# Pooling mixer of a diffusion trunk: rows scaled on ScalarE, the shift added by short matrix products

## The chip, the cores and the metric

The kernel runs on one core of a Trainium2 chip. The metric is the device time of one execution in microseconds (us); lower is better. TensorE is called PE in the rows below (PEld is its loading of the stationary operand), VectorE DVE, ScalarE ACT, GpSimd POOL, and SP is the queue that issues the loads.

## What is computed

Two layers over 512 latent tokens of width 1024 (and 256 context tokens in the first): layer 0 mixes tokens by attention, layer 1 by a pooling mixer, and each is followed by a gated feed-forward with a convolution. The change touches the seam from the feed-forward of layer 0 to that of layer 1, where this is computed:

```python
def rmsnorm(x, g):                       # over the 1024 channels of a token
    y = x * rsqrt(mean(x * x) + EPS); return y * g
def modulate(h, shift, scale): return h * (1.0 + scale) + shift

# layer 1, mixer: h = modulate(rmsnorm(x, g_pre_mix), shift_m, scale_m)
# four groups of 256 channels, windows w = 2, 4, 8, 16
pooled = mean of h over [t - w/2, t + w/2) (clipped to the sequence) - h[t]
y = (pooled @ w_pool[g] + b_pool[g]) * pool_scale
x = x + gate_m * rmsnorm(y, g_post_mix)
h = modulate(rmsnorm(x, g_pre_ffn), shift_f, scale_f)      # input of the second feed-forward
```

For a token in the middle of the sequence the window weights sum to one, so mean minus token gives zero for anything that is the same at every token, the shift among it. Within 8 tokens of either end that need not hold.

## The kernel before

Tokens lie in four tiles t of 128 partitions (`x[0]` to `x[3]`, full precision); the eight PSUM banks are four pairs `B2[0]` to `B2[3]` (printed as b1, b2, b3, b0 in this order). The second product of the first feed-forward (`down(0, ...)`, lines L122 to L124, three products of the split halves of both operands for each block) ends tile after tile, and `after_ffn0(t)` follows each:

- `post_norm` (L249 to L254): squares of the row on ScalarE (L167), the mean on VectorE (L168, L169), the power -1/2 on GpSimd (L151), then the residual is added on VectorE (L251, L254).
- the pre-norm of layer 1: again L167, L168, L169 and L151, then on VectorE `h = x * Arow` (L876, two halves of 512 columns) and `h = h * r + Brow` (L878, two halves). `Arow` and `Brow` hold gain and shift, copied to all 128 partitions by `to_row` (L207).
- `band(half, s)` (L844): products of `hx[s]` with columns of `bandt`, a matrix that holds the window weights minus one on the diagonal, with different columns for the first, the inner and the last tile. They run in full precision, and the trace has two records for each: 46 products in the program, 92 records.
- `pooled(half)` splits the sums into two parts `hTp` (cast on ScalarE, L128; rest on VectorE, L129). `mix(t)` multiplies with the pool weights (L122 to L124) and adds the bias (L861), then does `post_norm`. `mixed(t)` is `pre_norm(t, ...)` for the second feed-forward: L167 to L151, row scaling on VectorE (L231, into `mixrow`), eight transposes on TensorE (L234), gain and shift on VectorE for the first half (L239) and on ScalarE for the second (L242), and the split into `hT` (L128, L129), on which the first products of the second feed-forward (`up7`) wait.

After tile 3 come `mix(0)`, `mix(1)`, the remaining bands, `pooled(1)`, `mixed(0)`, `mixed(1)`, `mix(2)` and `mix(3)`; `mixed(2)` and `mixed(3)` are called inside `up7`. A scheduler of the framework places the instructions on each engine's queue; each queue runs in order.

Of the kernel before, what the change touches and what calls it, by code (L numbers as in the profile page):

```python
# [13 lines left out]
AF = mybir.ActivationFunctionType  # L14
ALU = mybir.AluOpType
AX = mybir.AxisListType

P = 128
D = 1024
SEQ = 512  # L20
CTX = 256
KT = D // P
TT = SEQ // P
# [15 lines left out]

HALO = 8  # L40

BI, BE = P + 2 * HALO, P + HALO
BW = BI + 2 * BE
NSLOT = 64

PE_TILE = 5
# [3 lines left out]
def trunk(ctx: ExitStack, tc: tile.TileContext, a, out: bass.AP):  # L50
    nc = tc.nc
# [35 lines left out]
    def rows(name, i, n=2, dt=F32):  # L87
        return flat(slots(name, i, n, dt))
# [111 lines left out]
    def gate_col(i, n):  # L200
        V.tensor_mul(Gcol[:, i, n, :], mods[:, i, 3 * n + 2, :], gcols[:, 2 + n, i, :])

    def to_row(dst, col):

        d = dram.tile([KT, P], F32, tag="bounce", name="bounce")
        nc.sync.dma_start(out=d.rearrange("j p -> p j"), in_=col)
        nc.sync.dma_start(out=dst, in_=d.rearrange("j p -> (j p)").unsqueeze(0).broadcast_to([P, D]))  # L207

    bg = []

# [10 lines left out]
    def halves(z):  # L221
        return [z[:, c] for c in HALVES]

    def pre_norm(t, pair, xn, A, Bc, h32=h32):


        r = rstd_halves(halves(x[t]), xn)
        ps = [z.rearrange("p (j s) -> p j s", s=P) for z in pair]
        sl = slice(t * P, (t + 1) * P)
        for c in range(2):  # L230
            V.tensor_scalar(xn[:, HALVES[c]], x[t][:, HALVES[c]], r, None, op0=ALU.mult)  # L231
            for j in range(4):
                f = 4 * c + j
                T.transpose(ps[c][:, j, :], xn[:, f * P:(f + 1) * P], ident)  # L234
        for c in range(2):
            for j in range(4):
                f = 4 * c + j
                if c == 0:
                    V.tensor_scalar(h32[:, f, :], ps[c][:, j, :], A[:, f:f + 1], Bc[:, f:f + 1],  # L239
                                    op0=ALU.mult, op1=ALU.add)  # L240
                else:
                    S.activation(h32[:, f, :], ps[c][:, j, :], AF.Identity, bias=Bc[:, f:f + 1], scale=A[:, f:f + 1])  # L242
        for c in range(2):
            k = slice(4 * c, 4 * c + 4)
            split(hT[:, k, sl], hT[:, KT + 4 * c:KT + 4 * c + 4, sl], h32[:, k, :])
# [552 lines left out]
    Gm1 = flat(cvt)  # L798
    hall = slots("hall", 52, KT, F32)
    wpl_dst = [[rows(f"wpl{n}{z}", i + 2 * z, dt=F32R) for z in range(2)] for n, i in enumerate((16, 20))]  # L800
    Arow, Brow = rows("Arow", 24), rows("Brow", 26)
    bandt = rows("band", 28, 4)[:, :4 * BW].rearrange("p (g b) -> p g b", g=4)
    hTp = [[slots(f"hTp{n}{z}", (32, 44)[n] + 4 * z, 4) for z in range(2)] for n in range(2)]
    wtail = [tuple(rows(f"wtail{n}{z}", 4 * n + 2 * z, dt=F32R) for z in range(2)) for n in range(4)]
# [24 lines left out]
    def band(half, s, groups=range(4)):  # L829
# [8 lines left out]
        for g in groups:  # L838
            if at == 256 and g == 0:
                continue  # L840
            ps = B2[2 * half + g // 2][g % 2].rearrange("p (k s) -> p k s", k=2)
            for k in range(2):
                f = slice((2 * g + k) * P, (2 * g + k + 1) * P)
                T.matmul(ps[:, k, lo:hi], hx[s][:, f], bandt[:, g, b0:b0 + hi - lo],  # L844
                         start=at == 0 and k == 0, stop=False, skip_group_check=True)

    def pooled(half):
        hi, lo = (z.rearrange("p a (j s) -> p (a j) s", s=256) for z in hTp[half])
# [15 lines left out]
        mixrow.append(row)  # L864

    def mixed(t):
        pre_norm(t, B2[t], mixrow[t], Acol[:, 1, 1], mods[:, 1, 3], hall[:, :, t * P:(t + 1) * P])

    def after_ffn0(t):
        if t == 1:  # L870
# [4 lines left out]
        for c in HALVES:  # L875
            V.tensor_mul(h[:, c], x[t][:, c], Arow[:, c])  # L876
        for c in HALVES:
            V.scalar_tensor_tensor(h[:, c], h[:, c], r, Brow[:, c], op0=ALU.mult, op1=ALU.add)  # L878
        hx.append(h)
        if t == 1:  # L880
            band(0, 0)
# [20 lines left out]
    def each0(c, kk):  # L902
# [5 lines left out]
            ps_row.append(pool_bias())  # L908
        if c == 1 and kk == FT // 2 - LAST:
            to_row(Arow, Acol[:, 1, 0, :])  # L910
            to_row(Brow, mods[:, 1, 0, :])
            pool_weights(ps_row[0])

    def down(i, aT, done, each, last, dst=(), order=(2, 3, 0, 1)):
# [32 lines left out]
def _constants():  # L947

    f = np.float32
# [14 lines left out]
    for g, w in enumerate(WINDOWS):  # L964
# [2 lines left out]
        e = m - np.eye(SEQ, dtype=f)  # L967
        band[:, g, :BI] = e[P:2 * P, P - HALO:2 * P + HALO]
        band[:, g, BI:BI + BE] = e[:P, :BE]
        band[:, g, BI + BE:] = e[SEQ - P:, SEQ - BE:]  # L970
    return rope, band


# [53 lines left out]
```

## Time and profile before

| | |
|---|---|
| runs | 1074.54, 1069.29, 1071.18 us; median 1071.18 |
| profiled execution | 1074.04 us, of which the span from first to last instruction is 1072.3 |
| busy share of the span | PE 93%, VectorE 70%, ScalarE 48%, GpSimd 3% |
| chain that ended last | PE 56%, VectorE 18%, DMA 12%, ScalarE 8% |
| mean granted TensorE clock | 0.977 of full speed |

The profiled execution is 2.86 us above the median of the runs. A difference that is worked out on its trace is therefore added to the median. The seam that the change touches lies between 648 and 730 us of the span.

### The profile page before, as it was taken

To read this page: it belongs to the slowest core of one execution; us is meant where nothing else is said; L and a number is where in the kernel's file an instruction comes from. 1 tells how busy PE (TensorE), PEld (TensorE's weight loads), DVE (VectorE), ACT (ScalarE), POOL (GpSimd) and SP (SyncE) were. 2 spreads that over 40 slices of the span, in tenths; PEclk is the share of its full clock that TensorE was granted. 3 is DMA by queue.
4 is the path that set the end of the run, shared out by engine and by line. 5 is a ranking of instruction groups with operands and counts; after the bars stand their busy time and mean duration, and the time that the engine had idled before them with its cause. 6 is when DMAs were issued, how large, how long until landed. Compare 5 with 4: busy or idle time off the path is not lost.

```text
span 1072.3 us, 14605 instructions
## 1 busy us (share of the span) xinstructions
PE 997.8 (93%) x5586; PEld 862.9 (80%) x5586; DVE 747.6 (70%) x1259; ACT 511.4 (48%) x986; POOL 37.5 (3%) x55
## 2 busy tenths in 40 slices
PE   0898889999979999989999999899999999999997
PEld 0666678788878888878888887788999999988885
DVE  3988777896777999565542236889799999982214
ACT  5658578865624333244331223555455555761111
POOL 2003000000000000000000001110000000000000
PEclk9999899999989999989999999989999999999999
DMA  8543431352189989744333353411132332043312
GB/s 316 193 150 98 154 92 70 118 159 77 40 274 247 335 316 338 134 104 138 98 114 102 99 180 106 133 45 40 60 118 81 118 107 91 21 157 99 99 59 78
DMA packets 46778, 143.70 MB, mean 134 GB/s; under 512 B 11122, under 2 KB 11506, under 8 KB 46708
## 3 DMA queue, kind: packets, MB, share of 16 engines
q1 hardware_dynamic: 46708, 142.77, 41.4%
q8 instruction: 43, 0.70, 0.3%
q14 instruction: 27, 0.22, 0.1%
HBM read 140.63 MB, written 2.12 MB: 133 GB/s over the span
## 4 chain that ended last, share of the span: by engine, by line
PE 56%; DVE 18%; DMA 12%; ACT 8%; issue 4%; POOL 2%; SPq 0%; DVEq 0%; ACTq 0%; POOLq 0%
PE b L124 11%; PE b L122 11%; PE b L123 11%; PE b L733 5%; DMA mraw<-in_w_mod 5%; PE b L734 5%; DVE mraw L186 5%; PE b L735 5%; DVE wlo L129 3%; DMA raw<-in_w_up 2%; POOL rr L151 2%; DMA bpr<-in_b_pool 1%; DMA bounce<-Gcol 1%; DMA raw<-in_w_o 1%; DVE x L254 1%
## 5 line engine op out<-in xcount | busy, mean ns | idle before, releaser
L129 DVE TENSOR_TENSOR wlo<-raw,whi 128x1024 fp32r<-128x1024 f32 x105 | 128.0, 1223 | 150.2 <-ACT whi L128 150.0
L128 ACT CAST whi<-raw 128x1024 fp32r<-128x1024 f32 x105 | 110.1, 1053 | 178.9 <-PE b L124 105.1
L122 PE MATMUL b<-hT,whi 128*128 128x512 f32 (+1 forms) x480 | 175.5, 367 | 7.4 <-ACT hT L128 5.2
L123 PE MATMUL b<-hT,whi 128*128 128x512 f32 (+1 forms) x480 | 175.5, 366 | 0.6 <-DVE hT L129 0.6
L124 PE MATMUL b<-hT,wlo 128*128 128x512 f32 (+1 forms) x480 | 175.4, 366 | 0.6 <-DVE wlo L129 0.6
L122 PE MATMUL b<-whi,a 128*128 128x512 f32 x320 | 124.6, 390 | 0.8 <-ACT whi L128 0.8
L123 PE MATMUL b<-wlo,a 128*128 128x512 f32 x320 | 124.6, 389 | 0.3 <-DVE wlo L129 0.3
L124 PE MATMUL b<-whi,a 128*128 128x512 f32 x320 | 124.4, 389 | 0.0
L186 DVE CUSTOM_DVE_ANT_0 mraw<-mraw,scrow,bmod 128x1024 f32<-128x1024 f32 x80 | 101.2, 1281 | 14.8 <-DMA mraw<-in_w_mod 14.6
L122 PEld LDWEIGHTS b<-hT,whi 128*128 128x128 f32 x480 | 92.4, 193 | 22.3 <-ACT hT L128 5.6
L124 PEld LDWEIGHTS b<-hT,wlo 128*128 128x128 f32 x480 | 92.4, 193 | 15.1 <-DVE wlo L129 1.3
L123 PEld LDWEIGHTS b<-hT,whi 128*128 128x128 f32 x480 | 92.4, 192 | 15.0 <-DVE hT L129 1.1
L733 PE MATMUL b<-hT,whi 128*128 128x256 f32 x288 | 81.9, 285 | 0.1
L735 PE MATMUL b<-hT,wlo 128*128 128x256 f32 x288 | 81.5, 283 | 0.0
L734 PE MATMUL b<-hT,whi 128*128 128x256 f32 x288 | 81.4, 283 | 0.0
L151 POOL TENSOR_TENSOR rr<-rv,mhalf 128x1 f32<-128x1 f32 (+2 forms) x48 | 36.7, 768 | 1029.4 <-DVE rv L169 854.6
L122 PEld LDWEIGHTS b<-whi,a 128*128 128x128 f32 x320 | 60.0, 188 | 13.9 <-ACT whi L128 1.2
L123 PEld LDWEIGHTS b<-wlo,a 128*128 128x128 f32 x320 | 60.1, 188 | 13.3 <-DVE wlo L129 0.7
L124 PEld LDWEIGHTS b<-whi,a 128*128 128x128 f32 x320 | 60.1, 188 | 12.2
L733 PEld LDWEIGHTS b<-hT,whi 128*128 128x128 f32 x288 | 55.2, 192 | 1.0 <-ACT gates L762 0.9
L734 PEld LDWEIGHTS b<-hT,whi 128*128 128x128 f32 x288 | 55.2, 192 | 0.0
L735 PEld LDWEIGHTS b<-hT,wlo 128*128 128x128 f32 x288 | 55.2, 192 | 0.0
(307 smaller groups left out, 2162.4 us busy)
## 6 DMA issues: line engine op xcount, KB each, us to landing
mraw<-in_w_mod SPq DMA_DIRECT2D x96, 512.0 KB, 5.1
raw<-in_w_up SPq DMA_DIRECT2D x52, 512.0 KB, 4.0
raw<-in_w_down SPq DMA_DIRECT2D x44, 512.0 KB, 3.4
upv<-in_w_up SPq DMA_DIRECT2D x18, 512.0 KB, 4.1
upg<-in_w_up SPq DMA_DIRECT2D x18, 512.0 KB, 3.5
raw<-in_w_qkv SPq DMA_DIRECT2D x12, 512.0 KB, 4.3
raw<-in_w_o SPq DMA_DIRECT2D x8, 512.0 KB, 3.5
x<-in_x SPq DMA_DIRECT2D x4, 512.0 KB, 10.0
```

The costliest lines, as they stand in the source:

```text
L122: T.matmul(ps, lh, rh, start=first, stop=False)
L123: T.matmul(ps, lh, rl, start=False, stop=False)
L124: T.matmul(ps, ll, rh, start=False, stop=last)
L128: S.copy(hi, src)
L129: V.tensor_sub(lo, src, F(hi))
L151: G.tensor_tensor(r[:, :n], v, mhalf[:, :n], op=ALU.pow)
L186: V.tensor_tensor_reduce(raw, raw, scrow, 1.0, bias, ALU.mult, ALU.add, mods[:, i, v, j:j + 1])
L254: V.scalar_tensor_tensor(xc, row[:, HALVES[c]], r, xc, op0=ALU.mult, op1=ALU.add)
L733: T.matmul(ps, lhs[0], rhs[0], start=first and k == 0, stop=False, skip_group_check=True)
L734: T.matmul(ps, lhs[0], rhs[1], start=False, stop=False, skip_group_check=True)
L735: T.matmul(ps, lhs[1], rhs[0], start=False, stop=last, skip_group_check=True)
```

## The change

The scaling by `r` moves to ScalarE (`S.activation(..., AF.Copy, scale=r)`) in two places: in `after_ffn0`, where the shift is no longer added, and in `pre_norm` for the four calls from `mixed` alone. `Brow` becomes one row on one partition. The shift is brought in by short products: each band product of the first and of the last tile is followed by one with a single contraction row, `Brow` (1 x 128 of it as the stationary operand) with 8 columns that hold the sums of the window weights for the 8 tokens at that end. These sums are appended to row 0 of the band matrix, which grows from 416 to 432 columns a group. There are 8 short products for tile 0 and 8 for tile 3. VectorE loses L878 (8 instructions) and the eight of L231 that belong to `mixed`; ScalarE gets 16.

```diff
@@ -200,11 +202,11 @@
-    def to_row(dst, col):
+    def to_row(dst, col, n=P):
...
-        nc.sync.dma_start(out=dst, in_=d.rearrange("j p -> (j p)").unsqueeze(0).broadcast_to([P, D]))
+        nc.sync.dma_start(out=dst, in_=d.rearrange("j p -> (j p)").unsqueeze(0).broadcast_to([n, D]))
@@ -221,14 +223,17 @@
-    def pre_norm(t, pair, xn, A, Bc, h32=h32):
+    def pre_norm(t, pair, xn, A, Bc, h32=h32, on_act=False):
...
         for c in range(2):
-            V.tensor_scalar(xn[:, HALVES[c]], x[t][:, HALVES[c]], r, None, op0=ALU.mult)
+            if on_act:
+                S.activation(xn[:, HALVES[c]], x[t][:, HALVES[c]], AF.Copy, scale=r)
+            else:
+                V.tensor_scalar(xn[:, HALVES[c]], x[t][:, HALVES[c]], r, None, op0=ALU.mult)
@@ -798,7 +803,7 @@
-    Arow, Brow = rows("Arow", 24), rows("Brow", 26)
+    Arow, Brow = rows("Arow", 24), rows("Brow", 26)[0:1, :]
@@ -843,6 +848,11 @@
                 T.matmul(ps[:, k, lo:hi], hx[s][:, f], bandt[:, g, b0:b0 + hi - lo],
                          start=at == 0 and k == 0, stop=False, skip_group_check=True)
+                if s == 0 or s == TT - 1:
+
+                    e = 0 if s == 0 else HALO
+                    T.matmul(ps[:, k, (256 - HALO) * half:(256 - HALO) * half + HALO], Brow[:, f],
+                             bandt[0:1, g, BS + e:BS + e + HALO], start=False, stop=False, skip_group_check=True)
@@ -864,7 +874,7 @@
-        pre_norm(t, B2[t], mixrow[t], Acol[:, 1, 1], mods[:, 1, 3], hall[:, :, t * P:(t + 1) * P])
+        pre_norm(t, B2[t], mixrow[t], Acol[:, 1, 1], mods[:, 1, 3], hall[:, :, t * P:(t + 1) * P], True)
@@ -875,7 +885,7 @@
         for c in HALVES:
-            V.scalar_tensor_tensor(h[:, c], h[:, c], r, Brow[:, c], op0=ALU.mult, op1=ALU.add)
+            S.activation(h[:, c], h[:, c], AF.Copy, scale=r)
@@ -908,7 +918,7 @@
-            to_row(Brow, mods[:, 1, 0, :])
+            to_row(Brow, mods[:, 1, 0, :], 1)
@@ -967,7 +977,10 @@
+        left = e.astype(np.float64).sum(0)
...
+        band[0, g, BS:BS + HALO], band[0, g, BS + HALO:] = left[:HALO], left[-HALO:]
```

In the changed file the lines are later by up to 10: L122 to L124 are L124 to L126 there, L128 is L130, L167 is L169, L844 is L849; the short product is L854, the new scalings are L888 and L234.

The first place is TensorE where tile 0 reaches its bands (`hx_5167` is `hx[0]`, `wtail` and `a0` belong to the last products of the feed-forward). Before:

```order
L124 MATMUL b2_2708<-whi_5127,a0_0_21_2731 128x512
L844 MATMUL b1_2611<-band_4531,hx_5167 128x136 x4
L122 MATMUL b3_2709<-wtail00_4536,a0_1_10_2742 128x512
L123 MATMUL b3_2709<-wtail01_4537,a0_1_10_2742 128x512
L124 MATMUL b3_2709<-wtail00_4536,a0_1_10_2742 128x512
L122 MATMUL b3_2709<-wtail00_4536,a0_1_11_2743 128x512
```

Now (the two kinds of product take turns four times on each of b1 and b2):

```order
L126 MATMUL b2_2708<-whi_5127,a0_0_21_2731 128x512
L849 MATMUL b1_2611<-band_4531,hx_5167 128x136
L854 MATMUL b1_2611<-band_4531,Brow_4530 128x8
L849 MATMUL b1_2611<-band_4531,hx_5167 128x136
L854 MATMUL b1_2611<-band_4531,Brow_4530 128x8
...
L124 MATMUL b3_2709<-wtail00_4536,a0_1_10_2742 128x512
L125 MATMUL b3_2709<-wtail01_4537,a0_1_10_2742 128x512
```

Each band product on b1 and b2 now has a short one behind it; tile 3 has the same on b3 and b0. The second place is TensorE where tile 2 reaches its bands (`hx2`), with the last products of tile 3 around them (b0 from `a0`). Before:

```order
L124 MATMUL b0_2610<-whi_5121,a0_1_18_2750 128x512
L122 MATMUL b0_2610<-whi_5121,a0_1_19_2751 128x512
L123 MATMUL b0_2610<-wlo_5122,a0_1_19_2751 128x512
L844 MATMUL b1_2611<-band_4531,hx2_5306 128x8 x2
L844 MATMUL b3_2709<-band_4531,hx2_5306 128x136 x2
L844 MATMUL b2_2708<-band_4531,hx2_5306 128x8 x4
L844 MATMUL b3_2709<-band_4531,hx2_5306 128x136 x2
L844 MATMUL b3_2709<-band_4531,hx_5229 128x8 x4
L124 MATMUL b0_2610<-whi_5121,a0_1_19_2751 128x512
L122 MATMUL b0_2610<-whi_5127,a0_1_20_2752 128x512
```

Now:

```order
L126 MATMUL b0_2610<-whi_5121,a0_1_18_2750 128x512
L849 MATMUL b1_2611<-band_4531,hx2_5314 128x8 x2
L849 MATMUL b3_2709<-band_4531,hx2_5314 128x136 x2
L849 MATMUL b2_2708<-band_4531,hx2_5314 128x8 x4
L849 MATMUL b3_2709<-band_4531,hx2_5314 128x136 x2
L849 MATMUL b3_2709<-band_4531,hx_5229 128x8 x4
L124 MATMUL b0_2610<-whi_5121,a0_1_19_2751 128x512
L125 MATMUL b0_2610<-wlo_5122,a0_1_19_2751 128x512
L126 MATMUL b0_2610<-whi_5121,a0_1_19_2751 128x512
```

Two products of tile 3 that stood ahead of the bands stand behind them. The third place is ScalarE after tile 3 (`x0` and `x1` are the tokens of tiles 0 and 1 after their `mix`; `hTp10` is what `pooled(1)` writes). Before:

```order
L167 ACTIVATE mixrow_5442,ss2_5443<-b1_2611 128x512
L167 ACTIVATE mixrow_5483,ss2_5484<-b2_2708 128x512 x2
L128 CAST hTp10_4534<-b3_2709 128x512
L128 CAST hTp10_4534<-b0_2610 128x512
L167 ACTIVATE mixrow_5442,ss2_5520<-x0_108 128x512 x2
L167 ACTIVATE mixrow_5483,ss2_5550<-x1_109 128x512 x2
L128 CAST hTp10_4534<-b3_2709 128x512
L128 CAST hTp10_4534<-b0_2610 128x512
L242 ACTIVATE hall_4524<-b1_2611,mods_99,Acol_101 128x128 x4
```

Now:

```order
L169 ACTIVATE mixrow_5450,ss2_5451<-b1_2611 128x512
L888 ACTIVATE hx3_5397<-hx3_5397,rr_5416 128x512 x2
L169 ACTIVATE mixrow_5491,ss2_5492<-b2_2708 128x512 x2
L130 CAST hTp10_4534<-b3_2709 128x512
L169 ACTIVATE mixrow_5450,ss2_5536<-x0_108 128x512
L130 CAST hTp10_4534<-b0_2610 128x512
L169 ACTIVATE mixrow_5450,ss2_5536<-x0_108 128x512
L169 ACTIVATE mixrow_5491,ss2_5566<-x1_109 128x512 x2
L130 CAST hTp10_4534<-b3_2709 128x512
L130 CAST hTp10_4534<-b0_2610 128x512
L234 ACTIVATE mixrow_5450<-x0_108,rr_5542 128x512 x2
L234 ACTIVATE mixrow_5491<-x1_109,rr_5572 128x512 x2
L247 ACTIVATE hall_4524<-b1_2611,mods_99,Acol_101 128x128 x4
```

The cast of b0 now stands between the two squares of `x0` and ahead of those of `x1`; the scaling of `hx3` stands ahead of the squares of `mixrow` from b2, and the scalings of `x0` and `x1` ahead of L242 (L247 now). On VectorE the rows of L878 and L231 are gone from their places and the others keep their order, except that for tile 1 both L251 now stand behind L169.

## Rows read from the trace of the kernel before

**Rows 1.** Waits of PE from 655 us on: who waited for whom, total us, times, longest.

```profile
PE b L122 <- DVE hTp L129: 6.3, 1, 6.3
PE b L122 <- ACT hT L128: 1.3, 1, 1.3
PE b L844 <- DVE hx L878: 1.2, 3, 0.6
PE b L123 <- DVE hT L129: 0.6, 1, 0.6
```

**Rows 2.** Stretches: us, PE, PEld, DVE, ACT, POOL busy, then PEclk, DMA.

```profile
690.00:695.00 5.00, 2.34 (x19) 2.08 (x18) 4.87 (x12) 2.56 (x6) 0.90 (x2) 0.96 0.88 297
695.00:700.00 5.00, 1.34 (x6) 1.34 (x6) 4.46 (x11) 2.39 (x6) 0.73 (x3) 0.50 0.72 279
700.00:705.00 5.00, 4.71 (x23) 4.42 (x23) 3.72 (x11) 0.93 (x3) 0.58 (x2) 0.51 0.00 2
```

**Rows 3.** Timeline of PE: start us, us, records merged, [idle before, ended by].

```profile
664.24 2.12 PE L844 MATMUL b<-band,hx 128*128 128x136 f32 x16 [0.41 <-DVE hx L878]
...
676.91 3.30 PE L844 MATMUL b<-band,hx 128*128 128x8 f32 x28 [0.56 <-DVE hx L878]
680.06 0.48 PE L124 MATMUL b<-whi,a 128*128 128x512 f32 x1
...
688.25 0.28 PE L861 MATMUL b<-bp,ones 128*128 128x256 f32 x1
688.37 4.00 PE L844 MATMUL b<-band,hx 128*128 128x136 f32 x32
698.66 0.58 PE L122 MATMUL b<-wpl,hTp 128*128 128x256 f32 x1 [6.29 <-DVE hTp L129]
...
700.60 3.68 PE L234 MATMUL b<-ident,mixrow 128*128 128x128 f32 x16 [0.29 <-DVE mixrow L231]
```

**Rows 4.** Timeline of PE around the only 2-row products.

```profile
57.45 0.39 PE L123 MATMUL b<-wkvl,hT 128*128 128x512 f32 x1
57.68 0.40 PE L124 MATMUL b<-wkvh,hT 128*128 128x512 f32 x1
58.01 0.28 PE L313 MATMUL b<-ident,modrow 2*128 2x2 f32 x2
58.22 0.50 PE L122 MATMUL b<-wkvh,hT 128*128 128x512 f32 x1
58.55 0.39 PE L123 MATMUL b<-wkvl,hT 128*128 128x512 f32 x1
```

**Rows 5.** Timeline of ACT: what those 2-row products waited for.

```profile
57.22 0.36 ACT L310 COPY modrow<-b 2x256 f32<-2x256 f32 x1 [3.82 <-PE b L309]
```

**Rows 6.** Timeline of DVE behind tile 3, and in the second norm of tile 3.

```profile
689.38 1.42 DVE L878 SCALAR_TENSOR_TENSOR hx<-hx,rr,Brow 128x512 f32<-128x512 f32 x2 [0.44 <-POOL rr L151]
...
695.24 1.42 DVE L254 SCALAR_TENSOR_TENSOR x<-mixrow,rr,x 128x512 f32<-128x512 f32 x2
696.57 1.28 DVE L129 TENSOR_TENSOR hTp<-b,hTp 128x512 fp32r<-128x512 f32 x2
...
718.78 0.88 DVE L231 TENSOR_SCALAR mixrow<-x,rr 128x512 f32<-128x512 f32 x2 [0.73 <-POOL rr L151]
```

**Rows 7.** Timeline of ACT behind tile 3.

```profile
692.41 0.59 ACT L128 CAST hTp<-b 128x512 fp32r<-128x512 f32 x1 [0.34 <-PE b L844]
...
696.08 0.63 ACT L167 ACTIVATE mixrow<-x 128x512 f32<-128x512 f32 x1 [1.60 <-DVE x L254]
...
697.32 1.15 ACT L128 CAST hTp<-b 128x512 fp32r<-128x512 f32 x2
```

**Rows 8.** ACT by form: count, busy us, mean ns, idle before.

```profile
L515 ACT ACTIVATE p<-p,ri 128x768 f32<-128x768 f32 x32 | 29.9, 936 | 0.5 <-DVE ri L514 0.5
L455 ACT ACTIVATE qr<-qr,rr 128x128 f32<-128x128 f32 x32 | 10.4, 395 | 5.2 <-DVE qr L404 5.1
```

**Rows 9.** Line L231: ns min/median/max, first and last start.

```profile
L231 DVE TENSOR_SCALAR mixrow<-x,rr x10: 478/482/486, 307.4 to 719.2; 128x512 f32<-128x512 f32 x10
```

More of the change, by code (lines that the diff above doesn't have):

```diff
@@ L42 @@
 BI, BE = P + 2 * HALO, P + HALO
-BW = BI + 2 * BE
+BS = BI + 2 * BE
+BW = BS + 2 * HALO
 NSLOT = 64
@@ L969, in _constants @@
         band[:, g, BI:BI + BE] = e[:P, :BE]
-        band[:, g, BI + BE:] = e[SEQ - P:, SEQ - BE:]
+        band[:, g, BI + BE:BS] = e[SEQ - P:, SEQ - BE:]
+        left = e.astype(np.float64).sum(0)
+        assert not left[HALO:-HALO].any()
+        band[0, g, BS:BS + HALO], band[0, g, BS + HALO:] = left[:HALO], left[-HALO:]
     return rope, band
```

## The prediction

> **What bounds the kernel now.** The page comes first. TensorE is busy nearly all the time and holds over half of the chain that ended last, so the question is where it is not busy, and whether the change reaches those places. The waits of TensorE [rows 1] answer that. From 655 us to the end it lacks input for over nine microseconds in the seam: 6.3 us for VectorE's half of the split `hTp`, 1.3 and 0.6 us for `hT`, and 1.2 us in three pieces for `hx`. Outside the seam a shift is passed on to the end unchanged, since TensorE is the one that is waited for there. [...] The idle time begins at 692.37 (688.37 + 4.00) and ends at 698.66 [rows 3]. So VectorE looks like the bound of the seam. But its queue is fed by others: the second pair of `hTp` on VectorE follows casts on ScalarE that begin at 697.32 [rows 6, 7]. And ahead of that, between 655 and 692 us, TensorE is the one that is always late, and there the change adds work.
>
> **What a short product costs.** Sixteen are new, eight behind tile 0 and eight behind tile 3, each between two band products. No product of one row stands in the trace. The nearest are the only products of two rows [rows 4]: their form is 2*128 where all neighbours are 128*128. From the start of L124 at 57.68 to the start of the second product behind them at 58.55 pass 0.87 us. Two undisturbed products take 0.46 (0.23 from 57.45 to 57.68, twice). The two records with the change of form and the way back thus cost 0.41 us. They did not wait for their input: ScalarE had it ready at 57.58 [rows 5], and L124 would have made room at 57.91. A short product in full precision is two records as well (the 46 band products have 92), so I take 0.41 us for one. Change of precision is not what costs: the full-precision bands at 688.37 start 0.12 us behind the product at 688.25 [rows 3], at the pace of the records around it. The low end is a short product that costs nothing but its records: 28 records, most of 8 columns, take 3.15 us (676.91 to 680.06) [rows 3], so two take 0.23. Below that it can't go, as these records are the smallest of this precision on the trace. The high end adds the two, 0.64: the records hide nothing under the change of form. I take 0.41, as its row contains a change of form and the other does not.
>
> [...]
>
> **Tile 0.** Eight short products are 8 x 0.41 = 3.28 us more on TensorE, on the path, since tile 2's last product stands behind them in the same queue. The wait of 0.41 us ahead of tile 1's bands [rows 3] is swallowed, which leaves 2.87. The scaling itself is no slower: an ACTIVATE with its factor in a column takes 0.395 us for 128 columns and 0.936 for 768 [rows 8], so 0.395 + 384/640 x 0.541 = 0.72 for 512, against 0.71 for one of the two halves of L878 (1.42 for both) [rows 6]. Tile 2's norm then starts 2.87 us later, and its bands at 676.91 + 2.87 = 679.78. Two products of tile 3 (0.46 us) now stand behind these bands, so TensorE reaches them early and waits about 1.0 instead of 0.56 us. The product that stood at 680.06 starts at 679.78 + 3.15 + 0.46 = 683.39. Tile 3's chain is late by 3.33 us.
>
> **Tile 3.** Counted from there, VectorE loses L878 (1.42 us) [rows 6], the gain that the change has to offer: L254 of `x1` and the first pair of `hTp` could come 1.4 us earlier. But ScalarE's queue decides. The cast of b0 was released by the bands at 692.41 [rows 7]. Now eight short products stand ahead of it, so it begins at 692.41 + 3.28 = 695.69. Behind it in the queue are a square of `x0` (0.63), two of `x1` (1.24, from 696.08 to 697.32) and then the second pair of casts, so 695.69 + 0.57 + 0.63 + 1.24 = 698.13, where they began at 697.32: 0.8 later, and VectorE's 1.42 is spent in waiting. The scaling of `x0` follows the same chain, on ScalarE in 0.72 instead of 0.48 us [rows 9], which is 0.24 more for the transposes. Its second half is not late, as four transposes take 0.92 (3.68/16 each) [rows 3]. So 3.33 + 0.8 + 0.24 = 4.4 us for the transposes that were at 700.60, and for the work of TensorE behind them. What was queued behind the new instructions on ScalarE is covered: the scaling of `hx3` is over at 689.38 + 1.33 and the squares behind it at 692.0, where the first cast has to wait for its bands anyway.
>
> **The second norm of tiles 2 and 3.** L239 of tile 2 stood on VectorE behind L231 of tile 3, with its wait of 0.73 and its 0.88 us [rows 6]. Both go, 1.61. Against that ScalarE takes 1.33 instead of 0.89 for tile 2's two halves, and the last four transposes (about 0.5) are no longer hidden. This returns about 0.6 us, and shortens the waits of 1.3 and 0.6 us for `hT` [rows 1].
>
> **Priced at nothing.** The load of `Brow` shrinks from 128 rows to one and that of the band matrix grows by 4%; no wait in rows 1 is for a DMA, and both are issued long before the seam. If the band matrix came late, tile 0's bands would wait by the same 4% of its load. VectorE's other order for tile 1 is hidden: its L251 then stand behind a mean that comes earlier than before.
>
> **Sum.** 2.87 + 0.46 + 0.8 + 0.24 - 0.6 = +3.8 us. On the profiled execution that is 1074.04 + 3.8 = 1077.8, and on the median 1071.18 + 3.8 = 1075.0, which I give. [...]
>
> **Rival one: the short products cost only their records.** For it speaks that both kinds have full precision and 128 columns of stationary operand. At 0.23 us: 1.84 - 0.41 + 0.46 = 1.89 for tile 3's start; the cast of b0 at 694.25 and the second pair at 696.69, 0.6 us earlier than before; + 0.24 - 0.6. That is +0.9 us, 1072.1, or 1071.2 with the clock up. Here the relief of VectorE comes through, and still the work added at tile 0 takes it back. Chance 0.22.
>
> **Rival two: ScalarE's queue behind the short products makes it clearly slower.** Each tenth of a microsecond of a short product is paid twice, eight times ahead of tile 2's chain and eight times ahead of the cast of b0, on which the squares of `x1` depend only by the queue. At 0.64 us: 5.12 + 0.05 = 5.17 for tile 3's start, the cast of b0 at 697.53, the second pair at 699.97 (+2.65), + 0.24 - 0.6: +7.5 us, 1078.6. It is 16 us of time for each microsecond of price, so the bound of 0.5% (5.4 us, about what a measurement of this kernel tells from no change) is passed from 0.51 us for a short product. For it speaks that rows 4 have one change of form alone, not eight in a row. Against it: nothing in rows 4 exceeds 0.41. Chance 0.18.
>
> **How the numbers follow.** Forecast, between about +2 and +5.3 us: chance 0.60. Range: the first rival with its clock and the scatter of the medians (the runs shown lie within 1069.29 and 1074.54) gives 1070.0 below; the second gives 1079.0 above. Slower by over 0.5%: most of rival two and the edge of the forecast, 0.22. Faster by over 0.5%: no term reaches -5.4 us, so only scatter, 0.03. Within 0.5%: 0.75.
>
> **What would show it.** [...] Wrong would be: band products and short ones at one pace, or ScalarE idle between 693 and 698.

## The result, and the profile after

| | before | after |
|---|---|---|
| runs | 1065.49 to 1075.68 us, median 1070.05 of 12 | 1074.47 to 1088.98 us, median 1083.19 of 12 |
| profiled execution (span) | 1074.04 us (1072.3) | 1076.36 us (1074.6) |
| PE busy, mean granted clock | 93%, 0.977 | 94%, 0.975 |
| chain that ended last | PE 56%, VectorE 18% | PE 73%, VectorE 8% |

The changed kernel takes 1.0092 times as long, 95% interval 1.0063 to 1.0121: some 10 us, where 3.8 were forecast. (The two medians of the table lie 13.1 us apart, a little more than the interval of the ratio allows; either way the time, 1083.19 us, lies above the range, which ended at 1079.0.) It is slower by over 0.5%, which had a chance of 0.22.

The two profiled executions differ by 2.3 us only, which misleads. That of before lost time far ahead of the change (TensorE waits 2.18 us up to 465.7 us, with a granted clock of 0.59 and 0.73 in the two stretches of 5 us behind it), and that of after did not; it reaches the first band product 9 us sooner, and some 6 of these are won there. A wait of 2.2 to 7.3 us at this place, with half the clock around it, stands in 17 of the 18 traces of this case, so it is this one trace of the changed kernel that is the exception. All landmarks below are therefore counted from the first band product, which in the kernel before is this row of TensorE's timeline (start us, us, records merged, idle time ahead and what ended it):

```profile
656.71 1.19 PE L844 MATMUL b<-band,hx 128*128 128x136 f32 x8 [0.22 <-DVE hx L878]
```

From there to the first transpose of the second norm it took 700.60 - 656.71 = 43.89 us [rows 3]. TensorE's timeline of the changed kernel, at tile 0, at tile 2's bands, and from tile 3's last products to the transposes:

```profile
647.47 0.50 PE L849 MATMUL b<-band,hx 128*128 128x136 f32 x2 [0.51 <-ACT hx L888]
647.90 0.38 PE L854 MATMUL b<-band,Brow 1*128 1x8 f32 x2
648.21 0.50 PE L849 MATMUL b<-band,hx 128*128 128x136 f32 x2
...
673.83 3.34 PE L849 MATMUL b<-band,hx 128*128 128x8 f32 x28 [0.89 <-ACT hx L888]
...
692.82 0.50 PE L849 MATMUL b<-band,hx 128*128 128x136 f32 x2
693.25 0.38 PE L854 MATMUL b<-band,Brow 1*128 1x8 f32 x2
693.56 0.50 PE L849 MATMUL b<-band,hx 128*128 128x136 f32 x2
693.99 0.54 PE L854 MATMUL b<-band,Brow 1*128 1x8 f32 x2
694.46 0.82 PE L849 MATMUL b<-band,hx 128*128 128x136 f32 x2
695.21 0.59 PE L854 MATMUL b<-band,Brow 1*128 1x8 f32 x2
699.52 0.58 PE L124 MATMUL b<-wpl,hTp 128*128 128x256 f32 x1 [3.72 <-DVE hTp L131]
...
701.69 3.23 PE L239 MATMUL b<-ident,mixrow 128*128 128x128 f32 x16 [0.30 <-ACT mixrow L234]
```

From band to band pass 0.74 us (647.47 to 648.21, 692.82 to 693.56). The last pairs are longer (0.82 and 0.59 us instead of 0.50 and 0.38): the clock falls before TensorE has done its last band. The transposes come 701.69 - 647.47 = 54.22 us from the first band, 10.33 later than before. The stretches show where the granted clock is down (us, busy time of PE, PEld, DVE, ACT, POOL, then PEclk):

```profile
650.00:655.00 5.00, 5.00 (x14) 3.86 (x14) 3.42 (x8) 2.39 (x6) 0.99 (x2) 0.50 0.04 17
655.00:660.00 5.00, 5.00 (x23) 4.01 (x22) 0.00 (x0) 0.33 (x1) 0.00 (x0) 0.85 0.00 0
...
675.00:680.00 5.00, 5.00 (x28) 4.42 (x27) 2.21 (x4) 2.45 (x5) 0.00 (x0) 0.70 0.00 0
...
690.00:695.00 5.00, 5.00 (x26) 4.04 (x26) 4.11 (x8) 1.86 (x6) 0.55 (x1) 0.91 0.40 149
695.00:700.00 5.00, 1.28 (x6) 0.98 (x5) 1.98 (x5) 3.39 (x9) 0.00 (x0) 0.50 0.60 211
700.00:705.00 5.00, 4.70 (x26) 4.40 (x26) 1.76 (x9) 2.56 (x4) 1.07 (x2) 0.57 0.26 104
```

Before, the clock was down in the last two of these only [rows 2]. Now it is at 0.50 behind tile 0's first bands as well, with TensorE busy 5.00 of 5 us, and again behind tile 2's (0.50 from 677.0 to 680.0, which the stretch shows as 0.70). TensorE's waits from 640 us on (who waited for whom, total us, times, longest):

```profile
PE b L124 <- DVE hTp L131: 3.7, 1, 3.7
PE b L124 <- ACT hT L130: 1.8, 1, 1.8
PE b L849 <- ACT hx L888: 1.4, 2, 0.9
PE b L125 <- DVE hT L131: 0.6, 1, 0.6
```

They sum to 7.5 us, and those of before to 9.4 [rows 1]. TensorE waits less and ends later. ScalarE's casts of `hTp` behind tile 3, and VectorE's part of it, in the same view:

```profile
692.18 0.59 ACT L130 CAST hTp<-b 128x512 fp32r<-128x512 f32 x1 [1.53 <-PE b L854]
695.84 0.59 ACT L130 CAST hTp<-b 128x512 fp32r<-128x512 f32 x1 [2.45 <-PE b L854]
...
698.17 1.06 ACT L130 CAST hTp<-b 128x512 fp32r<-128x512 f32 x2
```

```profile
696.46 0.69 DVE L131 TENSOR_TENSOR hTp<-b,hTp 128x512 fp32r<-128x512 f32 x1 [2.19 <-ACT hTp L130]
698.77 1.29 DVE L131 TENSOR_TENSOR hTp<-b,hTp 128x512 fp32r<-128x512 f32 x2 [1.56 <-ACT hTp L130]
```

VectorE, which was busy 4.87 and 4.46 of 5 us here before [rows 2], now waits 2.19 and 1.56 us for ScalarE, and ScalarE 1.53 and 2.45 us for the short products (L854). What the change gave VectorE is lost to waiting.

### The profile page after: what moved, and what is told of

Its sections match the earlier page's. It is cut to its first block, busy times and chain, and to the rows that moved or that the text cites. A ratio compares the mean times of both kernels' runs of the same rounds, so it can differ in the third digit from the quotient of the medians.

```text
span 1074.6 us, 14677 instructions
## 1 busy us (share of the span) xinstructions
PE 1006.4 (94%) x5618; PEld 870.3 (81%) x5618; DVE 738.6 (69%) x1243; ACT 521.0 (48%) x1002; POOL 37.4 (3%) x55
## 3 DMA queue, kind: packets, MB, share of 16 engines
HBM read 140.14 MB, written 2.12 MB: 132 GB/s over the span
## 4 chain that ended last, share of the span: by engine, by line
PE 73%; DVE 8%; ACT 7%; DMA 7%; issue 2%; POOL 1%; SPq 0%; DVEq 0%; ACTq 0%; POOLq 0%
PE b L124 17%; PE b L126 16%; PE b L125 16%; PE b L738 5%; PE b L739 4%; PE b L740 4%; DMA mraw<-in_w_mod 2%; PE b L849 1%; DMA upv<-in_w_up 1%; DVE wlo L131 1%; POOL rr L153 1%; DMA raw<-in_w_up 1%; PE tp L530 1%; DVE mraw L188 1%; DMA bounce<-Gcol 1%
## 5 line engine op out<-in xcount | busy, mean ns | idle before, releaser
L130 ACT CAST whi<-raw 128x1024 fp32r<-128x1024 f32 x105 | 110.0, 1052 | 179.3 <-PE b L126 106.1
L124 PE MATMUL b<-hT,whi 128*128 128x512 f32 (+1 forms) x480 | 174.9, 366 | 5.7 <-ACT hT L130 5.7
L126 PE MATMUL b<-hT,wlo 128*128 128x512 f32 (+1 forms) x480 | 174.9, 365 | 0.0
L124 PE MATMUL b<-whi,a 128*128 128x512 f32 x320 | 125.5, 393 | 1.1 <-ACT whi L130 1.1
L126 PE MATMUL b<-whi,a 128*128 128x512 f32 x320 | 124.8, 391 | 0.0
L124 PEld LDWEIGHTS b<-hT,whi 128*128 128x128 f32 x480 | 92.3, 193 | 19.8 <-ACT hT L130 6.2
L126 PEld LDWEIGHTS b<-hT,wlo 128*128 128x128 f32 x480 | 92.3, 192 | 13.6
L124 PEld LDWEIGHTS b<-whi,a 128*128 128x128 f32 x320 | 60.4, 189 | 14.3 <-ACT whi L130 1.5
L126 PEld LDWEIGHTS b<-whi,a 128*128 128x128 f32 x320 | 60.5, 189 | 12.6
```

The source lines that it names most:

```text
L124: T.matmul(ps, lh, rh, start=first, stop=False)
L126: T.matmul(ps, ll, rh, start=False, stop=last)
L130: S.copy(hi, src)
```

## The experiments

Three theories were put up at first. **A:** the change of form between products over 128 rows (`128*128` in the timelines) and over one row (`1*128`) costs, directly and by the clock. **B:** any sixteen products more, ahead of ScalarE's casts, cost this. **C:** the scalings on ScalarE are to blame. Two came later: **D**, the second norm on ScalarE is a loss of its own, and **E**, a longer wait ahead of tile 2's bands lets the clock fall behind them. The short names are those of the runs. Ratios are to the kernel before in runs on the same chip, with the 95% interval. "Tile 2's bands" and "first transposes" are counted from the first band product; "down" means that the granted clock fell to 0.50 in or right behind tile 2's bands, "up" that it read 1.00 in the stretches there. In the kernels named with no_onact the second norm's scaling is back on VectorE, in those named with v2 tile 2's scaling of `hx` (in full128_v2 and no_short_v2 both).

| kernel | wait ahead of tile 2's bands | tile 2's bands at | clock behind them | first transposes at | ratio |
|---|---|---|---|---|---|
| before | 0.56 | 20.2 | up | 43.9 | 1 |
| changed (3 traces) | 0.89 | 26.4, 23.3, 23.2 | down, down, up | 54.2, 54.1, 49.9 | 1.0092, 1.0087, 1.0069 |
| no_onact | 0.89 | 23.3 | down | 52.2 | 1.0094 |
| after_v2 (2 traces) | 0.52 | 23.1, 24.7 | up, up | 49.4, 52.8 | 1.0068 |
| full128 | 0.89 | 21.0 | down | 47.6 | 1.0006 |
| full128_v2 | 0.52 | 20.9 | up | 43.8 | 1.0006 |
| grouped | 0.89 | 21.6 | up | 45.2 | 1.0021 |
| grouped_no_onact | 0.89 | 21.5 | down | 48.0 | 1.0030 |
| edge_ahead | under 0.2 | 21.1 | up | 45.7 | 1.0032 |
| tile0_only | 0.89 | 23.3 | down | 48.4 | 1.0030 |
| tile3_only | 0.89 | 20.5 | down | 48.5 | 1.0034 |
| no_short | 0.89 | 20.3 | up | 42.9 | 0.9994 |
| no_short_no_onact | 0.88 | 20.5 | down | 45.6 | 0.9997 |
| no_short_v2 | 0.52 | 20.4 | up | 42.5 | 0.9992 |
| before_onact | 0.56 | 20.2 | up | 44.1 | 0.9990 |

### The same products over 128 rows

```diff
-    Arow, Brow = rows("Arow", 24), rows("Brow", 26)[0:1, :]
+    Arow, Brow = rows("Arow", 24), rows("Brow", 26)
...
-            to_row(Brow, mods[:, 1, 0, :], 1)
+            to_row(Brow, mods[:, 1, 0, :])
...
-                             bandt[0:1, g, BS + e:BS + e + HALO], start=False, stop=False, skip_group_check=True)
+                             bandt[:, g, BS + e:BS + e + HALO], start=False, stop=False, skip_group_check=True)
```

`Brow` lies on all 128 partitions again, and each short product contracts 128 rows; the columns appended to the band matrix are zero in rows 1 to 127. The number of products, their columns and the queues stay.

> [...] Theory A (change of form): a band and a short one take 0.46 us together instead of 0.74, the granted clock does not fall behind tile 0's bands (655 us region stays at 1.00), and the time is 1 to 2 us over the kernel before (ratio 1.001 to 1.002). Theory B (sixteen more products ahead of ScalarE's casts cost this whatever their form): the ratio stays within 1.007 to 1.010 as in the changed kernel. Theory C (the scalings on ScalarE are to blame): as B, with the period at 0.46.

The ratio is 1.0006 (0.9983 to 1.0030). TensorE's timeline at tile 0:

```profile
656.93 0.50 PE L849 MATMUL b<-band,hx 128*128 128x136 f32 x2
657.27 0.28 PE L854 MATMUL b<-band,Brow 128*128 128x8 f32 x2
657.41 0.48 PE L849 MATMUL b<-band,hx 128*128 128x136 f32 x2
657.73 0.28 PE L854 MATMUL b<-band,Brow 128*128 128x8 f32 x2
657.87 0.48 PE L849 MATMUL b<-band,hx 128*128 128x136 f32 x2
```

From band to band it is now 0.46 us (657.41 to 657.87), not 0.74. Nothing but the form was altered (and the copies of `Brow`, for which nothing waits), so the way to the other form and back costs 0.28 us, sixteen times 4.5 us, and the rest of the loss goes with it. Theory A holds, B and C fall.

Where the time goes is seen at the loading of the stationary operand, here of the first short product in the changed kernel and then in this one:

```profile
647.90 0.29 PEld L854 LDWEIGHTS b<-band,Brow 1*128 1x128 f32 x2
```

```profile
657.16 0.31 PEld L854 LDWEIGHTS b<-band,Brow 128*128 128x128 f32 x2
```

Over 128 rows it begins 0.11 us ahead of its product (657.27), while the band product is still running. Over one row it begins only when its product does (647.90), and so does the load of the band product behind it (both at 648.21). At each of the eight changes of this block, from 647.90 to 650.97, the load begins with its product.

### One-row products in a row

```diff
             band(0, 0)
+            edge(0)
             band(0, 1)
...
             band(1, 3)
+            edge(1)
             pooled(1)
```

(`edge` issues the short products of one end, taken out of `band`, by groups of channels. In the queue they stand four in a row, twice, at tile 0, and eight in a row at tile 3.)

> The changed kernel with the one-row products of a call behind all of its band products, four in a row on each pair of banks: 4 changes to the other form and 4 back instead of 16 and 16. Theory A: of 16 x 0.28 us (0.51 less 0.23) a quarter is left, about 1.1 us, the clock does not fall behind tile 0, and the time is 2 to 3 us over the kernel before (1.002 to 1.003). If each one-row product is slow by itself, next to another one too, it stays near 1.009. Theories B and C: 1.007 to 1.010.

The ratio is 1.0021 (0.9999 to 1.0042), as theory A said. TensorE's timeline at tile 0:

```profile
657.93 1.19 PE L849 MATMUL b<-band,hx 128*128 128x136 f32 x8
659.06 1.05 PE L859 MATMUL b<-band,Brow 1*128 1x8 f32 x8
660.04 0.50 PE L124 MATMUL b<-wtail,a 128*128 128x512 f32 x1
```

Four one-row products take 0.98 us from the first to what follows, way back included, so 0.25 each. That is within 0.02 us of one over 128 rows (0.46 - 0.23). It is the alternation that costs.

### No short products, and the second norm alone

```diff
-                if s == 0 or s == TT - 1:
-
-                    e = 0 if s == 0 else HALO
-                    T.matmul(ps[:, k, (256 - HALO) * half:(256 - HALO) * half + HALO], Brow[:, f],
-                             bandt[0:1, g, BS + e:BS + e + HALO], start=False, stop=False, skip_group_check=True)
```

> The changed kernel without the sixteen short products, which leaves the shift out at the 8 tokens of either end; the scalings stay on ScalarE. Theories A and B: VectorE's 1.42 us at tile 3 and about 0.6 us of the second norm show as a gain, 0.24 us for the slower scaling off, so 1 to 2 us under the kernel before (0.998 to 0.999). Theory C: the time stays at 1.007 to 1.010.

The ratio is 0.9994 (0.9966 to 1.0022). Without the short products the rest of the change is worth nothing that can be measured; the first transposes come 1.0 us sooner.

In the kernel before, the flag of `pre_norm` and the call from `mixed` alone:

```diff
-            V.tensor_scalar(xn[:, HALVES[c]], x[t][:, HALVES[c]], r, None, op0=ALU.mult)
+            if on_act:
+                S.activation(xn[:, HALVES[c]], x[t][:, HALVES[c]], AF.Copy, scale=r)
+            else:
+                V.tensor_scalar(xn[:, HALVES[c]], x[t][:, HALVES[c]], r, None, op0=ALU.mult)
```

> The kernel before with the row scaling of its second norm alone moved to ScalarE. By the prediction's own terms -0.6 + 0.24, so the same within 0.5 us (ratio 0.9995 to 1.000). Theory C, if the second norm is where it comes from: up to 1.005 and longer waits of TensorE for hT.

The ratio is 0.9990 (0.9969 to 1.0011): the same. In its trace TensorE's wait for `hT` is 1.8 us where it was 1.3 [rows 1], as ScalarE now has the scalings ahead of its half of `hall`:

```profile
717.77 2.56 ACT L232 ACTIVATE mixrow<-x,rr 128x512 f32<-128x512 f32 x4 [0.40 <-POOL rr L151]
721.32 1.50 ACT L245 ACTIVATE hall<-b,mods,Acol 128x128 f32<-128x128 f32 x4 [0.99 <-DVE hall L242]
```

### The changed kernel again, and three kernels with the second norm's scaling on VectorE

The changed kernel as it is:

> The changed kernel once more, beside the others of this call: ratio 1.007 to 1.011, the half clock behind tile 0's bands again (655 us region), a band and a short one in 0.74 us at full clock. If the fall of the clock there was scatter of one execution, it is gone while the time stays; then theory A keeps only its 16 x 0.28 us.

The ratio is 1.0087 (1.0056 to 1.0119). The half clock behind tile 0's bands was absent this time (1.00 from 655 to 665 us), and the time stayed: that fall comes in some executions only, and the loss does not need it. The transposes come as late as in the first trace all the same (54.1 and 54.2), as the clock is down for longer behind tile 2's bands (0.61 and 0.70 in two stretches of 5 us, 0.70 and 0.96 in the first trace) and at tile 3 (0.50 from 700 to 710).

```diff
-        pre_norm(t, B2[t], mixrow[t], Acol[:, 1, 1], mods[:, 1, 3], hall[:, :, t * P:(t + 1) * P], True)
+        pre_norm(t, B2[t], mixrow[t], Acol[:, 1, 1], mods[:, 1, 3], hall[:, :, t * P:(t + 1) * P])
```

This edit alone:

> The changed kernel with the row scaling of the second norm back on VectorE; the scaling of hx and the short products stay. Theory D: the second norm on ScalarE is a loss of 1.2 us (the wait of TensorE for hT grew from 1.3 to 1.8 us when that alone was moved, and the granted clock behind it fell), so the ratio is 0.001 under the changed kernel's, and the wait for hT is back at 1.3. The prediction's step: a loss of 0.6 us more without it.

The ratio is 1.0094 (1.0065 to 1.0122). The wait for `hT` is back at 1.3 us, but no time is gained. An interval of 0.003 on either side is too wide for the 0.001 of theory D; but of the four pairs of kernels that differ by this move alone (this one, before and before_onact, and the two below), none goes the way of theory D by its ratio: the scaling on ScalarE is level or lower each time, by 0.0003 to 0.0010. The wait is real; 0.4 of its 0.5 us are covered by what the move saves ahead of it (24.5 instead of 24.9 us from the first transposes to the wait).

The same edit in `grouped`, and then in `no_short`:

> One-row products four in a row, and the second norm's scaling on VectorE: the two repairs together. Theories A and D: 1.0021 less 0.0012, so 1.001, within 2 us of the kernel before; no half clock behind tile 0, full clock behind the last wait for hT.

The ratio is 1.0030 (1.0004 to 1.0057), not below `grouped`. The clock tells why this trace is later (stretches of `grouped` first, then two of this kernel, from tile 2's bands on):

```profile
680.00:685.00 5.00, 5.00 (x37) 4.59 (x37) 2.22 (x4) 3.04 (x6) 0.00 (x0) 1.00 0.00 0
```

```profile
676.00:681.00 5.00, 5.00 (x31) 4.71 (x31) 1.98 (x3) 1.87 (x4) 0.00 (x0) 0.72 0.00 0
681.00:686.00 5.00, 5.00 (x23) 4.42 (x22) 3.04 (x6) 3.73 (x7) 0.11 (x1) 0.60 0.29 93
```

Up to tile 2's bands the two run alike (21.6 and 21.5 us); the first transposes come at 45.2 and 48.0. Full clock behind the last wait for `hT`, which was expected as well, did not come: it read 0.54 from 729.2 to 731.7.

> Only the scaling of hx on ScalarE is left of the change: no short products (the shift is left out at the 8 tokens of either end) and the second norm's scaling on VectorE. What the relief of VectorE alone is worth: 1.0 us at tile 3's transposes by the trace without short products, so 0.998 to 0.999. If VectorE's 1.42 us at tile 3 came through in full, 0.998 or less.

The ratio is 0.9997 (0.9976 to 1.0019). It is the same pair once more: 42.9 us without the fall, 45.6 with it. In both pairs the trace with the fall of the clock behind tile 2's bands has the transposes 2.7 us later. (The pairs differ by the second norm's scaling too, which moved them by 0.2 us between before and before_onact.)

### One end at a time, and the products issued ahead

```diff
-                if s == 0 or s == TT - 1:
+                if s == 0:
```

> The changed kernel with the one-row products of tile 0 alone; those of tile 3 are left out, and with them the shift at the last 8 tokens. Counted from the first band product to the first transpose of the second norm (43.9 us in the kernel before, 42.9 without any short product and with the clock up behind tile 2): theory A gives 2.9 us for tile 0's eight alternations, so 45.8, or 48.5 if the granted clock falls behind tile 2's bands (2.7 us in the two pairs of kernels that differ by it). Tile 3's bands at the pace of 0.116 us a record, and a ratio of 1.002 to 1.005. The prediction's sum with tile 0 alone: 2.9 + 0.46 at tile 3, less 1.4, so 1.002.

The ratio is 1.0030 (1.0006 to 1.0055), the transposes at 48.4 with the clock down behind tile 2, where 48.5 was expected for that case.

The other end alone (`if s == TT - 1:`):

> The changed kernel with the one-row products of tile 3 alone (the shift is left out at the first 8 tokens). From the first band to the first transpose: 42.9 plus 8 x 0.51 = 4.1 us and up to 1.9 for the half clock during the alternation, so 47 to 49, and 2.7 more if the clock falls behind tile 2's bands. Ratio 1.004 to 1.006. If tile 0 and tile 3 cost the same, the two runs are alike within 1 us; if each is paid in full, the two losses over no short products at all add up to that of the changed kernel (10 us).

The ratio is 1.0034 (1.0016 to 1.0052), the transposes at 48.5, with the clock down behind tile 2 as well; 49.7 was the least expected for that case. The ratio is below the 1.004 to 1.006 that was expected, too. The two ends cost alike. Their losses over `no_short` (0.36% and 0.40%) add up to 0.76%, against 0.75% to 0.98% for the changed kernel; each of them carries an interval of 0.2% to 0.3% on either side.

```diff
+            edge(0)
             band(0, 2)
...
+            edge(1)
             band(1, 3)
```

This in `grouped_no_onact`, with the products over 128 rows:

> The whole computation, mended: short products over all 128 rows, eight in a row and issued ahead of the bands that wait for hx (tile 0's ahead of tile 2's bands, tile 3's ahead of tile 3's), and the second norm's scaling on VectorE as before. Theory A: 16 x 0.224 = 3.6 us of products, of which 0.7 fill TensorE's wait for hx of tile 3, less 1.0 of VectorE's relief: +1 to +2 us, ratio 1.000 to 1.002, no better than the kernel before beyond the scatter. If the order of the short products behind tile 3's bands was what ScalarE's casts paid for, the first transpose comes 1 us or more ahead of that with 128-row products behind each band at equal clock.

The ratio is 1.0032 (1.0013 to 1.0051), a miss. The first transposes are at 45.7, no earlier than with the products behind their bands (43.8 in `full128_v2`, further down). The clock is up behind tile 2's bands in both, but not at tile 3. Here it falls among the last bands, in which no product changes the form and TensorE is busy all the time (the last sixteen band records, and the stretch around them):

```profile
695.42 3.25 PE L849 MATMUL b<-band,hx 128*128 128x136 f32 x16
```

```profile
695.00:698.00 3.00, 3.00 (x20) 3.00 (x20) 2.84 (x7) 1.46 (x5) 0.55 (x1) 0.70 0.55 199
```

At full clock sixteen such records take 2.12 us [rows 3], so 1.1 of the 1.9 us between the two is the clock's. That placing the short products ahead of the bands gains anything is not seen.

### The wait ahead of tile 2's bands

```diff
+            if t == 2:
+                V.tensor_scalar(h[:, c], h[:, c], r, None, op0=ALU.mult)
+            else:
                 S.activation(h[:, c], h[:, c], AF.Copy, scale=r)
```

In `no_short_no_onact`:

> No short products (the shift is left out at the 8 tokens of either end), scaling of hx on ScalarE except for tile 2, where VectorE does it in 0.48 us a half without the shift, and the second norm's scaling on VectorE. TensorE's wait ahead of tile 2's bands goes from 0.89 to some 0.3 us. Theory E: the longer wait there is what lets the granted clock fall behind tile 2's bands, so the clock stays at 1.00 there and the first transpose comes at 42.9 us from the first band (45.6 with the fall). If the fall comes from elsewhere, it is seen here as well, in about three of five executions as in the kernels with that wait. Ratio 0.998 to 0.999 without the fall.

The ratio is 0.9992 (0.9973 to 1.0011). The clock stayed up and the transposes came at 42.5, as theory E had it:

```profile
667.92 2.12 PE L849 MATMUL b<-band,hx 128*128 128x136 f32 x16 [0.76 <-ACT hx L886]
681.01 3.30 PE L849 MATMUL b<-band,hx 128*128 128x8 f32 x28 [0.52 <-DVE hx L884]
```

In the changed kernel:

> The changed kernel with the scaling of hx of tile 2 alone on VectorE (0.48 us a half, without the shift). Theory E: TensorE's wait ahead of tile 2's bands goes from 0.89 to 0.5 us, the granted clock stays at 1.00 behind them, and with the fall 2.7 us go plus 0.4 of the wait: ratio 1.006. Against it: half clock there all the same, and a ratio of 1.008 to 1.009.

The ratio is 1.0068 (1.0043 to 1.0093). The clock stayed up behind tile 2's bands, but the time is that of the changed kernel on the same chip, which follows. The gain that theory E expected does not show. It does not show in the other pairs either: no_short_v2 has 0.9992 and no_short_no_onact 0.9997, and full128_v2, at the end, 1.0006 as full128.

> The changed kernel beside the others on this chip: ratio 1.009, half clock behind tile 2's bands, as in its two traces so far.

The ratio is 1.0069 (1.0042 to 1.0097). This execution had no half clock behind tile 2's bands either, in spite of the wait of 0.89 us, and so shows the changed kernel at its plainest:

```profile
658.71 0.39 PE L849 MATMUL b<-band,hx 128*128 128x136 f32 x2
...
681.92 3.33 PE L849 MATMUL b<-band,hx 128*128 128x8 f32 x28 [0.89 <-ACT hx L888]
...
693.87 2.28 PE L849 MATMUL b<-band,hx 128*128 128x136 f32 x18
...
701.38 0.82 PE L849 MATMUL b<-band,hx 128*128 128x136 f32 x2
702.13 0.59 PE L854 MATMUL b<-band,Brow 1*128 1x8 f32 x2
706.44 0.58 PE L124 MATMUL b<-wpl,hTp 128*128 128x256 f32 x1 [3.72 <-DVE hTp L131]
708.61 2.76 PE L239 MATMUL b<-ident,mixrow 128*128 128x128 f32 x16 [0.30 <-ACT mixrow L234]
```

> A second trace of the changed kernel with tile 2's hx on VectorE. Theory E: full clock behind tile 2's bands again. One execution of two with the half clock would leave the wait as a matter of odds and not the cause alone.

The clock stayed up behind tile 2's bands again. It was down behind tile 0's first bands in this execution (0.56 and 0.75 in two stretches of 2.5 us), and tile 2's bands come 1.7 us later than in the other trace of this kernel; as much again is lost at tile 3.

In `full128`, with the second norm's scaling on VectorE:

> The whole computation: short products over all 128 rows behind each band, tile 2's hx and the second norm scaled on VectorE, ScalarE scaling hx of the other tiles. Theories A and E: no half clock behind tile 2's bands, first transpose 44.5 us from the first band (42.5 without short products, plus 16 x 0.223 less what fills waits), which is +0.6 us on the kernel before, so 0.999 to 1.001: level with the kernel before, no faster.

The ratio is 1.0006 (0.9986 to 1.0026). Its timeline of TensorE:

```profile
658.22 0.50 PE L849 MATMUL b<-band,hx 128*128 128x136 f32 x2 [0.63 <-ACT hx L891]
...
679.09 3.30 PE L849 MATMUL b<-band,hx 128*128 128x8 f32 x28 [0.52 <-DVE hx L889]
...
700.09 0.58 PE L124 MATMUL b<-wpl,hTp 128*128 128x256 f32 x1 [3.72 <-DVE hTp L131]
702.02 2.94 PE L239 MATMUL b<-ident,mixrow 128*128 128x128 f32 x16 [0.28 <-DVE mixrow L236]
```

The transposes come at 702.02 - 658.22 = 43.80 us, and 43.89 before. So the idea of the change breaks even once no product changes the form: TensorE's wait for `hTp` shrinks from 6.29 to 3.72 us, and the sixteen products use that up. No kernel here beats the one before by more than its interval.

## Why the prediction was wrong, point by point

**The price of a short product: a term that was mis-sized.** It was taken as 0.41 us, from one change of form between long products [rows 4]. Measured is 0.74 - 0.23 = 0.51 between band products. The statement "nothing in rows 4 exceeds 0.41" was true of rows 4 and did not hold where the two kinds take turns. By the prediction's own 16 us for each microsecond of price, 0.51 makes +3.8 + 1.6 = +5.4 us for the time, 6.0 for the transposes (the 0.6 of the second norm come behind them). The two traces without a fall of the clock ahead of tile 3 show 49.9 - 43.9 = 6.0 (after_third) and 5.5 (after_v2, which waits 0.4 us less for tile 2). That the formula meets 6.0 so well is luck in part. By it tile 3's bands start 8 x 0.51 - 0.41 + 0.46 = 4.1 us later and take 4.1 us more. In after_third they start 3.5 us later, counted from the first band (35.2 instead of 31.7), and take 4.8 more up to their last record (8.5 instead of 3.7), 0.9 of it by the clock, as the next point shows. So the structure of the sum held, and its input did not.

**The clock: the step that failed.** The prediction's sum has no term for the clock, and so kept the half clock of the kernel before, which lay behind TensorE's last band there (0.50 and 0.51 from 695 to 705 us) [rows 2]. In all seven traces in which the two kinds of product take turns at tile 3 it begins before the last of them, at 693.99 in the changed kernel's rows (1.00 up to 694, 0.53 from 694 to 695). (In edge_ahead it did so too, without a change of form, so the alternation is not the only thing that brings it.) From the first band record of this block (693.87) to the start of its last short one pass 8.5 us in after_third, where some 7.6 are due at full clock (16 records of the inner tiles at 0.116, seven periods of 0.74 and 0.56 within the eighth, an estimate from rows at full clock), so 0.9 us more; in the second trace of the changed kernel it is 9.5. Behind tile 0 the clock fell in 2 of 7 traces with alternation there and in none of 11 without. Behind tile 2 it fell in 8 of 11 traces with a wait of 0.89 us and in none of 7 with 0.56 or less. The first two traces of the changed kernel are 4.3 us later than the third at the transposes, and have these falls: the first at tile 0 and tile 2, the second at tile 2 and for longer at tile 3.

**What this leaves open.** The three sets of runs put the changed kernel 7 to 10 us over before by their ratios. With 6.0 explained by alternation and the half clock within it, 1 to 4 us are left for the falls behind tile 0 and tile 2, which come in some executions only, and for the one behind the wait for `hT` (below). That the wait of 0.89 us brings the fall behind tile 2 is likely by the count, and the four kernels that shortened it have none, but no pair of kernels that differ in that wait differs in time, so its share in the time isn't shown. Why it falls in one execution and not in the next is not settled.

**Tile 0: right by luck, with two errors that cancel.** Forecast +2.87 us for tile 2's bands; measured +3.0 (23.2 against 20.2). The price was too low, but without short products the wait ahead of tile 1's bands is 0.76 us (row of no_short_v2), not 0.41, and all of it was swallowed: after_third and the other traces with alternation at tile 0 show no wait there. The wait of "about 1.0" ahead of tile 2's bands measured 0.89.

**Tile 3: right in its mechanism.** By the forecast 3.33 + 3.28 us are added up to the last band and 4.4 up to the transposes, so the way between the two should shrink by 2.2 us. From the start of the last record of tile 3's block to the first transpose it was 8.5 us and is 6.2 (after_third). By its terms TensorE was to idle 6.29 + 0.8 - 3.28 = 3.8 us ahead of the first product on `hTp`; it idles 3.72. The cast of b0 stands ahead of the squares of `x1`, and VectorE idles in front of the second pair, both as the forecast had it. What it did not have is the clock that falls inside these bands.

**The second norm: no gain, and a fall of the clock that was overlooked.** Forecast -0.6 us. From the first transposes to the wait for `hT` the kernel before takes 24.9 us and before_onact 24.5. The wait itself was said to get shorter and got longer, 1.3 to 1.8 us. Behind it the clock falls to 0.50 in all 11 traces with this scaling on ScalarE (a mean of 0.52 from 727 to 730 us in before_onact), and in 3 of 7 with it on VectorE; in the kernel before it stays at 1.00. From the product that waited to the end pass 347.4 to 350.9 us in the 14 traces with that fall and 346.6 to 347.3 in the four without. So the traces have a loss of one to two microseconds here where -0.6 was forecast; before_onact at 0.9990 doesn't confirm it in the time.

**The rivals.** Rival one (no price for the form, +0.9 us) came true where the form was taken away: full128 at +0.6 us (0.9983 to 1.0030). Rival two (0.64 us, +7.5) came nearest to the measured time, but by luck in part: its price was too high by 0.13 us where the forecast's was too low by 0.10, and the clock made up the rest. Its argument, that rows 4 hold one change and not eight in a row, was the right one.

**The range.** It reached only to rival two at 1079. A second state of the clock was looked at on the side of a gain alone (rival one's 1071.2 "with the clock up"), though the kernel before had shown in its own seam that the clock can fall: to 0.50 where TensorE was busy 2.34 and then 1.34 of 5 us [rows 2]. No run shows the 0.9 us that rival one takes off for the clock: in the changed kernel the granted clock was still 0.50 from 699.5 to 704 us, and the sixteen transposes took 3.23 us, where they took 3.68 before [rows 3].

## What to carry to other kernels

A small product in another form than its neighbours is priced in the row in which it will stand: two kinds in turn cost 0.28 us a pair here, the same short products in a row 0.02 us. Where rows of zeros filled the short operand up to the form of its neighbours (full128), it cost 0.23 us, its records alone. And where work on TensorE is added or spread out, the clock behind it belongs into the range on the side of a loss too, since a fall that goes with a delay of 2.7 us came in 8 of 11 traces with a wait that was 0.3 us longer than before, though its share in the measured time stayed open.

## What the runs showed of the hardware

- One-row full-precision products (`1*128`, two records each) in a row took 0.25 us each with the way back (grouped), 128-row ones 0.23 (full128); in turn with `128*128` products they took 0.51 (changed kernel). In turn, the loading of the stationary operand did not begin ahead of its product (647.90 and 648.21 in the changed kernel); without a change of form it began 0.11 us ahead (657.16 in full128).
- The granted clock fell to 0.50 while the records show TensorE busy all the time: in the alternation (5.00 of 5 us from 650 to 655 in the changed kernel), and without a change of form too, in and behind tile 2's bands (5.00 of 5 us from 676 to 681, mean clock 0.72, in grouped_no_onact) and in tile 3's of edge_ahead (3.00 of 3 us from 695 to 698, mean clock 0.70). What brings the fall was not shown.
- With a fall behind tile 2's bands the transposes came 2.7 us later in two pairs of kernels; it came and went between executions of one kernel (down, down and up in the three traces of the changed one).
- Behind a wait of TensorE of 1.8 us for `hT` the clock fell to 0.50 in 11 of 11 traces, behind one of 1.3 us at the same place in 3 of 7.
